# Entry of a SwiGLU FFN: the norm ahead of most weight splits, and the first half's products for two pairs of blocks at the beginning

## The chip, the cores and the metric

One NeuronCore of one Trainium2 chip. The metric is the device time of one execution of the program, in microseconds (us). Three runs of the kernel before took 769.72, 771.16 and 771.29 us; their median is 771.16 us.

## The reference

A decoder layer on 512 tokens of 1024 features, all float32: a norm, a combined projection, two groups of heads (RWKV-7 time mixing and sparse attention), an output projection with a residual, and then a dense SwiGLU FFN of 2816 hidden features with a second residual and a last norm. What the change touches is the seam between the output projection and the FFN:

```python
h = h + jnp.concatenate([y_r, y_n], axis=-1) @ w_out[l]
h = h + swiglu(rms_norm(h, norm_ffn[l]), w_gate[l], w_up[l], w_down[l])
return rms_norm(h, norm_final)

def swiglu(x, w_gate, w_up, w_down):
    return (jax.nn.silu(x @ w_gate) * (x @ w_up)) @ w_down
```

## The kernel before

*Products in three matmuls.* Every float32 product runs as three matmuls on a rounded high part ("hi") and a remainder ("lo") of each operand (`mm3`, L163 to L165). `split` (L144, L146) makes the two parts: hi is a copy by ScalarE (ACT), lo a subtraction by VectorE (DVE).

*Output projection (`accumulate` with `w_out`, L1157).* All eight banks of PSUM hold one output: four tiles of 128 tokens, two banks each, tile 0 in the banks "s", tile 1 in "pj", tile 2 in "ra", tile 3 in "o" and "rb". The last two slices of `w_out` run tile by tile, so that tile 0 is finished first; behind each tile come the residual adds into `x2` (L1159) and one step of the FFN's norm.

*The norm (`ffn_norm`).* For each tile: a sum of squares and a root on ScalarE, a reciprocal and the scaled product on VectorE (L1072), eight transposes on TensorE into two banks of "s" (L1082), and a copy by ScalarE into `raw` (L1084). The tokens are taken in two halves, tiles 0 and 1 against tiles 2 and 3, and the features in two halves too. For tiles 0 and 1 the copied values are split into A11 and A12. For tiles 2 and 3, four sums and differences with the tile of the first half (L1095 to L1097, L1100) and five splits give S1, S2, S3, S4 and A22.

*The weights (`weight_side`).* The 22 blocks of 128 hidden features are done in 11 pairs q. For each pair the 256 columns of `w_gate` and `w_up` are loaded in halves of 512 rows, 512 KB each: b11, b21 (both `w_gate`) and b22 into buffers of the tag "wraw" by SyncE's (SP) queue; t1 and t3 first by SP and then with an accumulating transfer that GpSimd (POOL) issues (L1137, L1138), which adds the other matrix. For odd q, t1 to t3 lie in a buffer of the tag "L", for even q in three of "t4". VectorE adds t2 = t1 + b22 (L1141) and later t2 + b21 (L1146). Seven operands are split for each pair: B11, B21, T2, T1, T3, B22, T4. Their parts go to buffers of the tags "whi" and "wlo" in turn, two of each; those of pair 0 that are made first (two of them) go to "b8".

*The pairs (`prod`, loop over q).* Seven products make the two halves of gate and up for both halves of the tokens: B11 with A11, B21 with A12, T2 with S2, T1 with S1, T3 with S3, B22 with S4, T4 with A22; 24 matmuls of 256 columns each, into banks of "pj", "ra" and "s" in turn. The first two products need only tiles 0 and 1; the other five need all four. VectorE adds up the products (L1187 to L1205), ScalarE takes the Silu.

*Order.* The kernel is written in a layer that decides the order of instructions of each engine itself when the program is built: a planner goes through the instructions in time by its own estimate of their durations, and where several are ready on an engine, program order decides, except that what is traced under `tc.high_priority()` goes ahead. It also gives out the buffers of a tag; an instruction that needs a buffer waits until the last reader of the tile in it is done. On the chip each engine then takes its instructions strictly in the planned order. Before the change the weights' sums, accumulating transfers and splits are under `high_priority`, the norm is not. `ahead()` traces pair 0's weights before the last tiles of the output projection:

```python
def ahead():
    first.append(weight_side(0, 2))

norm = ffn_norm(lambda t: x2[:, t])
for t, banks in accumulate(*jit(...), w_out, 8, ahead):
    for f in range(2):
        sl = slice(f * 512, f * 512 + 512)
        DVE.tensor_add(x2[:, t, sl], banks[f], x2[:, t, sl])
    next(norm)
```

*Buffers.* "L" has four, "b8" six, "t4" four, "t2" three (its tiles: the junk of the sum of squares, the norm's s3, the products' u, g0 and v, and smaller tiles in all stages before), "wraw" three. `raw` and the A operands lie in "L" too.

## Time and profile before

| | us |
|---|---|
| median of three runs | 771.16 |
| the profiled execution | 770.73 |
| its span | 769.0 |
| TensorE busy in the span | 738.6 (96%) |
| VectorE busy | 543.3 (71%) |
| ScalarE busy | 381.5 (50%) |
| POOL busy | 160.0 (21%) |

The profile is of one execution; its times run from the start of the span, and what lies outside of the span is 1.7 us. PE is TensorE's matmuls, PEld its weight loads, DVE VectorE, ACT ScalarE. Matmuls are pipelined, so a row of a single one (0.28 us) is longer than the distance to the next (0.12 us). The output projection runs until about 404 us, the 11 pairs until about 641, `w_down` and the last norm fill the rest. A line such as L146 is that of a helper and stands for many tiles, so rows are told apart by the tile's tag: "L<-L" a split of the norm, "whi<-t", "wlo<-wraw" splits of weights; "t<-L" is s3.

### The profile page before, as it was taken

To read this page: it belongs to the slowest core of one execution; us is meant where nothing else is said; L and a number is where in the kernel's file an instruction comes from. 1 tells how busy PE (TensorE), PEld (TensorE's weight loads), DVE (VectorE), ACT (ScalarE), POOL (GpSimd) and SP (SyncE) were. 2 spreads that over 40 slices of the span, in tenths; PEclk is the share of its full clock that TensorE was granted. 3 is DMA by queue.
4 is the path that set the end of the run, shared out by engine and by line. 5 is a ranking of instruction groups with operands and counts; after the bars stand their busy time and mean duration, and the time that the engine had idled before them with its cause. 6 is when DMAs were issued, how large, how long until landed. Compare 5 with 4: busy or idle time off the path is not lost.

```text
span 769.0 us, 14989 instructions
## 1 busy us (share of the span) xinstructions
PE 738.6 (96%) x6093; PEld 648.1 (84%) x6093; DVE 543.3 (71%) x1052; ACT 381.5 (50%) x652; POOL 160.0 (21%) x258
## 2 busy tenths in 40 slices
PE   8999999998889999999996899999999999999996
PEld 7867888898877878867786899999999998888885
DVE  5488689789768987875659497888695994333235
ACT  7398643224277776676447344444443552233224
POOL 3210054058345542442001102020202000000000
PEclk9999999999989999999998999999999999999998
DMA  7722543100051000321218569696768444322102
GB/s 247 223 82 84 164 110 110 55 2 2 3 219 30 3 1 3 85 83 56 83 55 192 110 176 203 161 223 151 161 159 221 112 153 147 110 68 97 55 1 110
DMA packets 69243, 82.83 MB, mean 108 GB/s; under 512 B 4868, under 2 KB 62806, under 8 KB 69174
## 3 DMA queue, kind: packets, MB, share of 16 engines
q1 hardware_dynamic: 57558, 70.34, 28.5%
q0 software_dynamic: 11616, 11.54, 9.9%
q8 instruction: 48, 0.79, 0.4%
q14 instruction: 21, 0.17, 0.1%
HBM read 79.77 MB, written 2.10 MB: 106 GB/s over the span
## 4 chain that ended last, share of the span: by engine, by line
PE 74%; DVE 15%; DMA 6%; issue 2%; ACT 1%; POOL 0%; SPq 0%; DVEq 0%; POOLq 0%; ACTq 0%
PE ps_ra L165 7%; PE ps_ra L164 7%; PE ps_ra L163 6%; PE ps_pj L165 6%; PE ps_pj L163 6%; PE ps_pj L164 6%; PE ps_s L165 4%; PE ps_s L163 4%; PE ps_s L164 4%; PE ps_o L1001 3%; DVE wlo L146 3%; PE ps_pj L993 2%; DMA L<-in_w_up_dram 2%; DMA wraw<-in_w_up_dram 2%; DMA L<-in_w_gate_dram 2%
## 5 line engine op out<-in xcount | busy, mean ns | idle before, releaser
L144 ACT ACTIVATE whi<-wraw 128x1024 fp32r<-128x1024 f32 (+1 forms) x79 | 78.5, 1033 | 33.2 <-PE ps_s L165 8.2
L146 DVE TENSOR_TENSOR wlo<-wraw,whi 128x1024 fp32r<-128x1024 f32 (+1 forms) x62 | 77.7, 1284 | 14.9 <-ACT whi L144 11.3
L146 DVE TENSOR_TENSOR L<-b,L 128x512 fp32r<-128x512 f32 x24 | 16.2, 691 | 57.1 <-PE ps_rb L164 55.1
L990 POOL TENSOR_SCALAR whi<-whi,m,gates 128x128 f32<-128x128 f32 (+3 forms) x64 | 42.5, 679 | 36.9 <-DVE m L988 28.7
L144 ACT ACTIVATE L<-b 128x512 fp32r<-128x512 f32 x24 | 14.9, 632 | 70.0 <-PE ps_rb L164 65.1
L164 PE MATMUL ps_ra<-wlo,L 128*128 128x256 f32 (+1 forms) x140 | 47.6, 340 | 0.2 <-DVE wlo L146 0.2
L163 PE MATMUL ps_ra<-whi,L 128*128 128x256 f32 (+1 forms) x140 | 47.4, 340 | 0.2 <-ACT L L144 0.2
L165 PE MATMUL ps_ra<-whi,L 128*128 128x256 f32 (+1 forms) x140 | 47.0, 337 | 0.0
L165 PE MATMUL ps_pj<-whi,L 128*128 128x256 f32 (+1 forms) x140 | 46.3, 332 | 0.0
L164 PE MATMUL ps_pj<-wlo,L 128*128 128x256 f32 (+1 forms) x140 | 46.3, 331 | 0.0
L163 PE MATMUL ps_pj<-whi,L 128*128 128x256 f32 (+1 forms) x140 | 45.9, 332 | 0.0
L164 PE MATMUL ps_ra<-L,whi 128*128 128x256 f32 (+2 forms) x128 | 44.3, 346 | 1.0 <-DVE L L146 1.0
L163 PE MATMUL ps_ra<-L,whi 128*128 128x256 f32 (+2 forms) x128 | 44.1, 345 | 0.9 <-ACT L L144 0.9
L165 PE MATMUL ps_ra<-L,wlo 128*128 128x512 f32 (+2 forms) x120 | 41.2, 343 | 0.0
L987 ACT ACTIVATE whi<-whi,m 128x128 f32<-128x128 f32 (+3 forms) x64 | 35.4, 554 | 9.3 <-DVE m L986 8.1
L165 PE MATMUL ps_pj<-L,wlo 128*128 128x512 f32 (+1 forms) x112 | 38.8, 346 | 0.1
L163 PE MATMUL ps_pj<-L,whi 128*128 128x512 f32 (+1 forms) x104 | 36.3, 349 | 0.2 <-ACT whi L144 0.2
L164 PE MATMUL ps_pj<-L,whi 128*128 128x512 f32 (+1 forms) x104 | 35.9, 346 | 0.0
L986 DVE CUSTOM_DVE_ANT_0 whi<-ps_s,negb 128x128 f32<-128x128 f32 (+3 forms) x64 | 29.3, 484 | 5.9 <-PE ps_pj L993 2.5
L1137 POOL DMA_DIRECT2D t<-in_w_up_dram x6 | 7.9, 1322 | 115.1 <-DVE whi L146 50.4
L163 PEld LDWEIGHTS ps_ra<-whi,L 128*128 128x128 f32 x140 | 27.6, 197 | 3.1 <-ACT L L144 0.6
L164 PEld LDWEIGHTS ps_ra<-wlo,L 128*128 128x128 f32 x140 | 27.5, 196 | 3.0 <-DVE wlo L146 0.5
(627 smaller groups left out, 2462.4 us busy)
## 6 DMA issues: line engine op xcount, KB each, us to landing
wraw<-in_w_gate_dram SPq DMA_DIRECT2D x22, 512.0 KB
wraw<-in_w_down_dram SPq DMA_DIRECT2D x11, 1024.0 KB
wraw<-in_w_in_dram SPq DMA_DIRECT2D x9, 1024.0 KB
t<-in_w_up_dram POOLq DMA_DIRECT2D x12, 512.0 KB, 7.4
wraw<-in_w_up_dram SPq DMA_DIRECT2D x11, 512.0 KB
L<-in_w_up_dram POOLq DMA_DIRECT2D x10, 512.0 KB, 8.9
wraw<-in_w_out_dram SPq DMA_DIRECT2D x4, 1024.0 KB
wraw<-in_w_in_dram SPq DMA_DIRECT2D x6, 512.0 KB
```

The lines of the kernel that those rows point to most:

```text
L144: ACT.activation(hi, src, AF.Copy)
L146: (POOL if pool else DVE).tensor_sub(lo, src, hi.bitcast(F32))
L163: PE.matmul(o, lh, rh, start=start, stop=False)
L164: PE.matmul(o, lh, rl, start=False, stop=False)
L165: PE.matmul(o, ll, rh, start=False, stop=stop)
L986: DVE.tensor_tensor_reduce(pr[:, i], pS[:, i], negb[:, S - n:S], scale=-1.0, scalar=3e38, op0=OP.add, op1=OP.min, accum_out=m[:, i, 0:1])
L987: ACT.activation(pr[:, i], pr[:, i], AF.Exp, scale=-1.0, bias=m[:, i, 0:1], accum_out=m[:, i, 1:2])
L990: POOL.tensor_scalar(pr[:, i], pr[:, i], m[:, i, 2:3], gv[:, 1 + b0 + i, h:h + 1], op0=OP.mult, op1=OP.mult)
L993: PE.transpose(pT[:, j], prr[:, x, j * 128:j * 128 + 128], ident)
L1001: PE.matmul(po[q, 2 * g:2 * g + 2], vtok[:, j % (t + 1), b0 + j // (t + 1), g], pTs[:, par, j], start=False, stop=g == 1 and bs[-1] == 1 a ...
L1137: POOL.dma_start(t1, quarter(w_up, 0), accum_op=OP.add)
```

## The change

- The norm's steps and the residual adds in front of them run under `high_priority`. Before the output projection's last tiles only B11 and B21 of pair 0 are prepared; pair 1's B11 and B21 and the rest of pair 0 (T2, T1, T3, B22, T4) are traced behind the norm.
- At the beginning the products of the first half of the tokens (B11, B21) run for pair 0 and pair 1, then the five other products of pair 0, then those of pair 1. From pair 2 on the order is as before.
- A11 and A12 are split straight from PSUM; the copy into `raw` comes behind.
- s3 = a11 - a21 is subtracted by POOL instead of VectorE.
- "t2" has four buffers instead of three; two small tiles of pair 1 change places with it. The scratch for POOL's transfers is halved.

```diff
-    SB_BUFS = {"L": 4, "b8": 6, "t4": 4, "t2": 3, "wraw": 3, "whi": 2, "wlo": 2}
+    SB_BUFS = {"L": 4, "b8": 6, "t4": 4, "t2": 4, "wraw": 3, "whi": 2, "wlo": 2}
...
-                rv = raw[:, kh * HK:kh * HK + HK, tl]
-                ACT.activation(rv, p.rearrange("p (k n) -> p k n", n=128), AF.Copy)
+                rv, pv = raw[:, kh * HK:kh * HK + HK, tl], p.rearrange("p (k n) -> p k n", n=128)
                 if t < 2:
-                    put(("A11", "A12")[kh], rv)
+                    put(("A11", "A12")[kh], pv)
+                ACT.activation(rv, pv, AF.Copy)
...
-                DVE.tensor_sub(s3, a11, a21)
+                POOL.tensor_sub(s3, a11, a21)
...
+    class Weights:
+        def __init__(self, q):
...
+            nc.sync.dma_start(self.b11, quarter(w_gate, 0))
+            nc.sync.dma_start(self.b21, quarter(w_gate, 1))
...
+        def begin(self, tag=None):
+            with tc.high_priority():
+                self.put("B11", self.b11, tag)
+                self.put("B21", self.b21, tag)
+
+        def rest(self):
+            b22 = st([128, 2048], "wraw")[:, 0:1024].rearrange("p (k n) -> p k n", n=256)
...
+            nc.sync.dma_start(t1, self.quarter(w_gate, 0))
+            nc.sync.dma_start(b22, self.quarter(w_up, 1))
+            nc.sync.dma_start(t3, self.quarter(w_up, 0))
+            with tc.high_priority():
+                POOL.dma_start(t1, self.quarter(w_up, 0), accum_op=OP.add)
+                POOL.dma_start(t3, self.quarter(w_up, 1), accum_op=OP.add)
+                DVE.tensor_add(t2, t1, b22)
+                self.put("T2", t2)
+                self.put("T1", t1)
+                self.put("T3", t3)
+                self.put("B22", b22)
+                DVE.tensor_add(t2, t2, self.b21)
+                self.put("T4", t2)
...
     def ahead():
-        first.append(weight_side(0, 2))
+        ws[0] = Weights(0)
+        ws[0].begin("b8")
...
-        for f in range(2):
-            sl = slice(f * 512, f * 512 + 512)
-            DVE.tensor_add(x2[:, t, sl], banks[f], x2[:, t, sl])
-        next(norm)
+        with tc.high_priority():
+            for f in range(2):
+                sl = slice(f * 512, f * 512 + 512)
+                DVE.tensor_add(x2[:, t, sl], banks[f], x2[:, t, sl])
+            next(norm)
...
+    ws[1] = Weights(1)
+    ws[1].begin()
+    ws[0].rest()
+    first_products(0)
+    first_products(1)
+    last_products(0)
+    ws[1].rest()
+    last_products(1)
+    for q in range(2, NF // 2):
+        ws[q] = Weights(q)
+        ws[q].begin()
+        ws[q].rest()
+        first_products(q)
+        last_products(q)
...
-    nc = _bacc.Bacc("TRN2", target_bir_lowering=False, num_devices=1, dynamic_dma_scratch_size=4096)
+    nc = _bacc.Bacc("TRN2", target_bir_lowering=False, num_devices=1, dynamic_dma_scratch_size=2048)
```

`first_products(q)` holds the first two products of the old loop's body with their evictions, `last_products(q)` the other five.

## Rows read from the trace of the kernel before

**Rows 1.** Page, part 2: busy tenths of TensorE in 40 equal slices of the span.

```profile
PE   8999999998889999999996899999999999999996
```

**Rows 2.** Windows: each engine's busy us (instructions), granted clock, DMA share, GB/s.

```profile
400.00:420.00 20.00, 15.81 (x91) 14.15 (x89) 18.52 (x26) 15.17 (x26) 2.62 (x2) 0.83 0.70 171
420.00:440.00 20.00, 15.59 (x111) 14.98 (x112) 9.72 (x14) 8.41 (x11) 2.59 (x2) 0.91 0.61 119
440.00:460.00 20.00, 20.00 (x170) 20.00 (x169) 19.34 (x24) 8.95 (x10) 1.27 (x1) 1.00 0.57 146
...
412.00:414.00 2.00, 2.00 (x11) 2.00 (x11) 2.00 (x5) 0.90 (x2) 0.00 (x0) 0.50 1.01 236
```

**Rows 3.** Chain of waits, 380 to 450 us: start us, us on the chain, what.

```profile
408.66 1.14 DVE t L1146
409.80 0.61 DVE L L146
...
425.23 4.02 DMA L<-in_w_gate_dram
...
429.87 6.13 DMA L<-in_w_up_dram
...
437.22 1.23 DVE whi L146
```

**Rows 4.** Timeline of TensorE: start us, us, instruction, idle time before it, releaser.

```profile
403.65 1.03 PE L1082 MATMUL ps_s<-ident,b 128*128 128x128 f32 x8
...
410.45 0.58 PE L164 MATMUL ps_pj<-L,b 128*128 128x256 f32 x1 [1.85 <-DVE L L146]
...
411.04 0.41 PE L163 MATMUL ps_pj<-L,b 128*128 128x256 f32 x1
411.26 0.41 PE L164 MATMUL ps_pj<-L,b 128*128 128x256 f32 x1
...
438.49 0.39 PE L165 MATMUL ps_pj<-L,whi 128*128 128x256 f32 x1 [2.52 <-DVE whi L146]
...
461.12 0.28 PE L163 MATMUL ps_s<-L,whi 128*128 128x256 f32 x1
```

**Rows 5.** Timeline of VectorE, 400 to 471 us, same columns.

```profile
400.44 1.28 DVE L1072 SCALAR_TENSOR_TENSOR b<-L,ss,t 128x1024 f32<-128x1024 f32 x1 [0.42 <-PE ps_s L1082]
...
403.44 1.22 DVE L146 TENSOR_TENSOR wlo<-t,wlo 128x1024 fp32r<-128x1024 f32 x1
...
406.31 1.22 DVE L146 TENSOR_TENSOR wlo<-wraw,wlo 128x1024 fp32r<-128x1024 f32 x1
407.44 1.22 DVE L146 TENSOR_TENSOR whi<-t,whi 128x1024 fp32r<-128x1024 f32 x1
...
409.71 1.29 DVE L146 TENSOR_TENSOR L<-L 128x512 fp32r<-128x512 f32 x2
...
424.51 0.69 DVE L146 TENSOR_TENSOR b<-L,b 128x512 fp32r<-128x512 f32 x1
...
436.08 1.23 DVE L1141 TENSOR_TENSOR L<-L,wraw 128x1024 f32<-128x1024 f32 x1 [5.09 <-DMA L<-in_w_up_dram]
...
470.83 1.22 DVE L1141 TENSOR_TENSOR L<-L,wraw 128x1024 f32<-128x1024 f32 x1 [3.83 <-DMA L<-in_w_up_dram]
```

**Rows 6.** Timeline of ScalarE, same columns.

```profile
400.00 1.09 ACT L1084 ACTIVATE L<-ps_s 128x512 f32<-128x512 f32 x2 [0.18 <-PE ps_s L1082]
...
437.40 1.06 ACT L144 ACTIVATE wlo<-L 128x1024 fp32r<-128x1024 f32 x1 [3.10 <-DVE L L1141]
```

**Rows 7.** Timeline of POOL, 300 to 480 us, same columns.

```profile
305.68 1.04 POOL L884 TENSOR_TENSOR L<-L,cs 128x512 f32<-128x512 f32 x1 [2.87 <-DVE m L988]
...
462.71 1.29 POOL L1137 DMA_DIRECT2D L<-in_w_up_dram  x1 [7.74 <-DVE t L1205]
```

**Rows 8.** Timeline of SyncE's queue, same columns.

```profile
384.97 0.37 SPq L1121 DMA_DIRECT2D wraw<-in_w_gate_dram  x1
...
454.78 0.37 SPq L1123 DMA_DIRECT2D L<-in_w_gate_dram  x1
```

More of the change, by code (lines that the diff above doesn't have):

```diff
@@ L1172, in prod, with first_products @@
         return o
-    hid = []
-    for q in range(NF // 2):
+    hid, part = [], {}
+    def first_products(q):
         if q % 2 == 0:
-            h4 = st([128, 4, S], "b8") if q < NF // 2 - 1 else st([128, 2, S], "t4")
-        hq = h4[:, q % 2 * 2:q % 2 * 2 + 2]
-        hid += [hq[:, j] for j in range(2)]
-        w = weight_side(q) if q else first[0]
-        u, g0, v, u1 = (st([128, 2, 256], tag) for tag in ("t2", "t2", "t2", ("lora", "smask")[q % 2]))
-        p = prod(w["B11"], A["A11"])
+            part["h"] = st([128, 4, S], "b8") if q < NF // 2 - 1 else st([128, 2, S], "t4")
+        hq = part["h"][:, q % 2 * 2:q % 2 * 2 + 2]
+        hid.extend(hq[:, j] for j in range(2))
+        w = ws[q]
+        u, g0 = st([128, 2, 256], "t2"), st([128, 2, 256], "smask" if q == 1 else "t2")
+        p = prod(w.B11, A["A11"])
         with tc.high_priority():
             ACT.activation(u, p, AF.Copy)
-        p = prod(w["B21"], A["A12"])
+        p = prod(w.B21, A["A12"])
         with tc.high_priority():
@@ L1198, in hybrid_layer @@
             DVE.tensor_add(u1, p, v)
-        p = prod(w["B22"], A["S4"])
+        p = prod(w.B22, A["S4"])
         with tc.high_priority():
@@ L1202, in hybrid_layer @@
         DVE.scalar_tensor_tensor(hq[:, :, 0:256], v, -1.0, g0, op0=OP.mult, op1=OP.mult)
-        p = prod(w["T4"], A["A22"])
+        p = prod(w.T4, A["A22"])
         with tc.high_priority():
```

65 lines of the change are left out of this document (25 added, 40 removed).

## Prediction

> **What bounds the kernel now.** I read the views from coarse to fine. The page's second part comes first: TensorE is at nine tenths nearly everywhere, and around 400 to 440 us its row falls to 6 and 8 (slices 22 and 23 of 40) [rows 1]. The 20 us windows say what that hole is: 15.81 and 15.59 us of busy TensorE in 400 to 440, at granted clocks of 0.83 and 0.91, and 20.00 at 1.00 right behind it; in the hole VectorE is full first (18.52 of 20) and then half idle (9.72) [rows 2]. So the FFN is bound by TensorE once it runs, and its entry is bound by something else.
>
> What that is, the chain of waits tells [rows 3]. Up to the first product's second matmul it runs over VectorE, from one split of weights to the next and the sum for T4 (L1146, 408.66) to a split of the norm (409.80). The end of the hole hangs on a load at 425.23 (4.02 us), an accumulating transfer at 429.87 (6.13 us) and a split at 437.22.
>
> TensorE's timeline shows the holes themselves [rows 4]: the last matmuls of the stage before and tile 1's transposes end some 0.9 us after 403.65, the first product gets going at 410.45 after a last wait of 1.85 us for VectorE, and at 438.49 another wait of 2.52 us ends. Warm matmuls take 0.12 us each (170 in 20 us [rows 2]), those behind the first hole 0.21 (411.04, 411.26): the lower of the two levels of the clock, 0.50 granted in 412 to 414 [rows 2]. The first product of pair 2 starts at 461.12 [rows 4], so that is where pairs 0 and 1 have ended. From there on TensorE is dense, and I count a microsecond won at that point as one won at the end.
>
> What could be had at most: two pairs are 14 products of 24 matmuls, 336 x 0.12 = 40.3 us, and 16 transposes of the tiles 2 and 3 in two groups of some 0.9 us. From the end of tile 1's transposes (403.65 + 0.9 = 404.5) that would end at 446.6, 14.5 us ahead of 461.1.
>
> **The change, part by part.** *Opening.* Today tile 1's A11/A12 come last on VectorE: 409.71, behind T1 at 403.44, T2, B22 (406.31), T3 (407.44) and the sum for T4 [rows 3, 5]. Splits of 128x1024 are 1.13 us apart (406.31, 407.44); two operations of 128x512 take 1.29 us where one takes 0.69, so 0.60 each [rows 5]. Ahead of the norm these are 5 x 1.13 = 5.7 us that now come behind it. The split out of PSUM also takes one ScalarE copy out of the chain (two take 1.09 us, so 0.5 each) [rows 6]. Against that, the bank of "s" is held until the copy, the hi and the lo have all read it, some 0.6 us more; I let these cancel. Tile 1's transposes end at 404.5, a hi (0.5) and a lo (0.6) follow: the first product starts at 405.5 instead of 410.45 (bounds 404.5, where the planner puts those transposes into the stage before, and 407, if one more split of 1.13 us gets in between).
>
> *Four products instead of two.* B11 and B21 of pairs 0 and 1 need tokens of tiles 0 and 1 alone. 4 x 24 x 0.12 = 11.5 us and 1.8 us of transposes, all warm if nothing breaks it: 405.5 + 13.3 = 418.8. What lies beside it on VectorE, from the end of tile 2's norm at 400.44 + 1.2 = 401.6: four lo's of tiles 0 and 1 (2.4), two residual adds of tile 3 (1.2), eight operations of tile 2 (4.8), the norm and eight operations of tile 3 (1.3 + 4.8), B11 and B21 of pair 1 (2.3), T2 (1.1), one eviction (0.6): 18.5 us, to 420.1. So VectorE is as full as TensorE; the norm, which goes first, ends at about 420 instead of 425.1 (bounds 418 and 422). T2 x S2 needs the S2 of tile 3, three operations into its eight, and I take a wait of 1.0 us (0 to 3): pair 0's five other products run from 419.8 to 434.2 (5 x 24 x 0.12 = 14.4). Behind the norm VectorE owes T1, T3, B22, the sum for T4 and T4 (5.7) and nine evictions and products of halves (5.4): 11.1 us in 14.4, so no wait more, but no room either.
>
> *POOL instead of VectorE for s3.* Two subtractions of 128x512. POOL's nearest row is another two-input operation of that size: 1.04 us [rows 7], against 0.60. VectorE gets 1.2 us back, and the overwriting of a21 waits 0.4 us longer per tile, which other splits fill: nothing either way (bounds: 1.2 gained, 1 lost). The Trainium skill speaks against this move: "GPSIMD Engine Reference", section 8, has VectorE about twice as fast at elementwise work and the two sharing SBUF interfaces when VectorE reads two SBUF inputs, as nearly all of its operations here do. By that page an estimate would be 1.4 us for each and some waiting on top, at most 1 us later in all. What weighs more is the queue: POOL also issues the accumulating transfers, and s3 stands behind any of them that waits.
>
> *Weights of pair 0.* Its t1 and t3 come long ahead. Pair 1's b11/b21 take the slot of wraw before pair 0's b22, which moves to about 385, where today pair 1's go [rows 8]; landed by 393 even at the slow load below, it is wanted behind the norm, at about 415: nothing.
>
> *Pair 1's sums.* Its t1, t2, t3 live in a buffer of "L" that raw gives back only when the norm has ended: issue at 425.23 today, as the norm's last split (424.51, 0.69 us) has ended [rows 3, 5]. After: about 420. From there 4.0 us of load and 0.6 us to the accumulating issue [rows 3], or 7.9 us as for pair 3, which loads among other transfers (454.78 to 462.71) [rows 7, 8]; then 6.2 us (429.87 to the sum at 436.08) or 8.1 (462.71 to 470.83) [rows 3, 5, 7]; then the sum, a hi and a lo (1.2 + 1.0 + 1.2) [rows 5, 6]. T2 of pair 1 is there between 420 + 4.6 + 6.2 + 3.4 = 434.2 and 420 + 7.9 + 8.1 + 3.4 = 439.4. Until now nobody waited for this end of the chain but one split behind it in VectorE's order; with pair 1's first products spent early, TensorE has nothing else. Pair 2's loads come into the same microseconds, as buffers of pair 0 fall free, so I take 437, past the middle: a wait of 2.8 us (0 to 5). The Trainium skill points the same way and sharpens it: "DMA: Bandwidth & Descriptors", section "Issuing engines are not separate DMA queues", says that transfers issued by any engine run on the same 16 DMA engines and interleave. The trace agrees as far as 7.9 us beside 4.0 go; by that rule the slow end, 439.4, would hold, pair 2 would start 2.4 us later, and the time would be 764.3.
>
> *Sum.* Pair 1's last five products start at 437.0 and end at 451.4. One hole of such a length costs clock: 17 matmuls at 0.21 instead of 0.12 are 1.5 us; the hole of 2.5 us before 438.49 cost none (1.00 granted behind it), the longer one at the opening did [rows 2, 4]; I take 0.9. Pair 2 then starts at 452.3 instead of 461.1: 8.8 us. The profiled execution took 770.73 us, 0.4 under the median of 771.16: 770.7 - 8.8 = 761.9, 762.4 from the median; I say 762.
>
> *Small things.* One more buffer of "t2" serves the two u and g0 that now live at once; it is also used far ahead of the FFN, and the planner may place work there otherwise: 0, bounds 2 us either way, as TensorE's row has few gaps there to fill or to widen [rows 1]. POOL's scratch is halved: the pairs of accumulating issues in flight are two, no row shows a want of room; 0, or one more accumulating transfer of 6.2 to 8.1 us in series for t3 of an odd pair, which only pair 1 could feel.
>
> **The rivals.**
> *All of it is covered* (757): loads as quick as today's and the planner finds work for the hole. No wait for S2 or T2: 405.5 + 13.3 + 28.8 = 447.6, 13.5 us won. For it speaks that TensorE mixes products today; against it that VectorE's sum is already as long as TensorE's.
> *VectorE in its order* (767): today VectorE stood 5.1 us before the sum at 436.08, with T4's split of pair 0 behind it [rows 5]. The same order with a sum that is there at 436 instead of 434, the slow end: T4's lo 1.2 + 1.2 us later at 438.4, T4 and the five products 17.2 us to 455.6, clock 1.5: 457.1, 4 us won.
> *Slower* (773): on POOL, pair 2's second accumulating issue stands ahead of pair 1's first, and its load waits for a buffer of t4 that pair 0's T4 split gives back, at about 428.5 (420.1, the 5.7 us of splits, 2.7 of evictions). Then 428.5 + 7.9 = 436.4 to issue, 8.1 to land, 3.4 to T2, 14.4 and 1.5: 463.8, 2.7 us lost. It decides once pair 1's accumulating issue comes later than 461.1 - 1.5 - 14.4 - 3.4 - 8.1 = 433.7. For it: POOL waits for whole loads and for buffers now (t1 of pair 3, loading since 454.78, was taken up at 462.71) [rows 7, 8]. Against it: the time between 420 and 433.7 is long.
> *It doesn't do what it says* (771): program order and priority only break ties; if each engine's order comes out as now, with the split of T2 and T1 ahead of tile 1's, only POOL and the extra buffer remain.
>
> **How the numbers follow.** Forecast 0.53, all covered 0.14, VectorE's order 0.20, slower 0.07, no effect 0.06. The range takes in the covered case and the opening's early bound (14.5 us, 756) and, above, VectorE's order with the 2 us of earlier work: 756 to 769. The three runs lie 0.2% apart, so 1.5 us is what can be told from no change. Faster: the first three, 0.87, less a little for the third's tail: 0.86; within 0.2%: 0.06; slower: 0.08.
>
> **What would show it.** Right: the first product's matmuls run from about 405 and the clock stays up to 418; the norm's last split at about 420 with SP's load for L right behind it; one hole of TensorE ahead of pair 1's T2, ended by VectorE or that transfer; pair 2 starting at about 452. Wrong: a start of products after 408, a norm that ends after 423, a POOL queue in which s3 waits for a transfer, or a shift of more than 2 us before 390 us.

## The result, and the profile after

The changed kernel takes 779.09 us (median of four runs, 777.67 to 779.93), the kernel before 771.02 us beside it (four runs, 769.72 to 771.29). The ratio is 1.0106, with a 95% interval from 1.0087 to 1.0125: slower by 8 us, where 9 us less were forecast. The profiled execution after took 779.93 us, its span 778.2; before they were 770.73 and 769.0. In the experiments below single executions of e8, e10 and e12 took far longer (898, 1429 and 3975 us); the ratios leave these out.

To see where 9.2 us went I cut the profiled executions at three points of TensorE's timeline: the last matmul of w_out starts, the first matmul of w_down starts, the last one starts. What lies between the first two is called the FFN stage below. A fourth mark lies inside of it: pairs 0 and 1 are 336 matmuls, and the 337th matmul of the pairs starts 57.7 us after w_out's end before (461.12) and 60.9 after (467.61). The stretch up to it is called the entry.

| profiled execution | w_out ends at | FFN stage | of it the entry | w_down |
|---|---|---|---|---|
| before | 403.4 | 238.9 | 57.7 | 119.5 |
| after | 406.7 | 241.3 | 60.9 | 123.0 |
| difference | +3.3 | +2.4 | +3.2 | +3.5 |

So only 2.4 of the 9.2 us lie where the change was meant to win 8.8, and 6.8 lie in stages whose computation the change leaves as it was. The page's second part of after, TensorE's row in 40 slices, shows the entry in slices 22 to 24, now 8, 8 and 8 where they were 6, 8 and 9 [rows 1]: less deep, and longer.

```profile
PE   6999899998989999999998889999999999999996
```

The windows of after (busy us of PE, PEld, DVE, ACT, POOL; granted clock; DMA share; GB/s) answer [rows 2]. TensorE has more in 400 to 420 than before (17.18 against 15.81) and as much in 420 to 440, but stands 3.4 us in 440 to 460, where it was full. VectorE, full at first before, is at 12.07:

```profile
400.00:420.00 20.00, 17.18 (x90) 14.61 (x89) 12.07 (x15) 11.54 (x19) 2.60 (x2) 0.83 0.31 70
420.00:440.00 20.00, 15.47 (x126) 14.66 (x125) 14.72 (x22) 12.26 (x22) 2.74 (x3) 1.00 0.62 156
440.00:460.00 20.00, 16.56 (x120) 15.73 (x120) 14.51 (x17) 6.84 (x8) 2.58 (x2) 0.91 0.51 95
460.00:480.00 20.00, 20.00 (x171) 20.00 (x171) 14.62 (x17) 9.54 (x11) 2.58 (x2) 1.00 0.99 256
```

TensorE's timeline of after answers [rows 4] (start us, us, instruction, idle time before it and what ended it):

```profile
406.73 0.39 PE L165 MATMUL ps_rb<-whi,L 128*128 128x512 f32 x1
408.08 0.65 PE L1082 MATMUL ps_s<-ident,b 128*128 128x128 f32 x4 [0.96 <-ACT L L1086]
409.51 0.66 PE L1082 MATMUL ps_s<-ident,b 128*128 128x128 f32 x4 [0.78 <-ACT L L1086]
410.94 0.58 PE L163 MATMUL ps_pj<-L,b 128*128 128x256 f32 x1 [0.78 <-ACT L L144]
...
412.53 0.58 PE L164 MATMUL ps_pj<-L,b 128*128 128x256 f32 x1 [0.31 <-DVE L L146]
412.91 0.41 PE L165 MATMUL ps_pj<-L,b 128*128 128x256 f32 x1
...
425.88 1.06 PE L1082 MATMUL ps_s<-ident,b 128*128 128x128 f32 x8 [1.73 <-DVE b L1072]
...
454.14 0.39 PE L163 MATMUL ps_s<-L,wlo 128*128 128x256 f32 x1 [2.18 <-ACT wlo L144]
```

The transposes of tile 1 (408.08, 409.51) wait twice for ScalarE's copy out of the bank of "s" that they are to fill. The first product begins at 410.94, cold (0.41 for a matmul that takes 0.28 warm), and tile 2's transposes stand behind 22 of its matmuls, at 417.18. In the kernel before they stand ahead of it:

```profile
406.70 1.14 PE L1082 MATMUL ps_s<-ident,b 128*128 128x128 f32 x8 [2.01 <-ACT L L1084]
```

ScalarE's timeline of after has the copies that free the banks, the first of tile 0 and the two of tile 1:

```profile
407.44 0.58 ACT L1086 ACTIVATE L<-ps_s 128x512 f32<-128x512 f32 x1
...
412.51 1.20 ACT L1086 ACTIVATE L<-ps_s 128x512 f32<-128x512 f32 x2 [1.13 <-DVE L L146]
```

The first stands behind two splits of pair 1's weights (from 405.53), the other two behind VectorE's lo of tile 1.

VectorE's timeline of after answers [rows 5]:

```profile
408.39 1.22 DVE L146 TENSOR_TENSOR whi<-wraw,whi 128x1024 fp32r<-128x1024 f32 x1
409.52 1.22 DVE L146 TENSOR_TENSOR wlo<-t,wlo 128x1024 fp32r<-128x1024 f32 x1
410.66 1.22 DVE L146 TENSOR_TENSOR whi<-t,whi 128x1024 fp32r<-128x1024 f32 x1
411.79 1.28 DVE L146 TENSOR_TENSOR L<-ps_s,L 128x512 fp32r<-128x512 f32 x2
...
420.05 0.69 DVE L1096 TENSOR_TENSOR L<-L 128x512 f32<-128x512 f32 x1 [5.84 <-POOL t L1095]
...
435.33 0.69 DVE L146 TENSOR_TENSOR b<-L,b 128x512 fp32r<-128x512 f32 x1
```

Splits of weights still stand in front of tile 1's part of A11 and A12 (411.79); VectorE then waits 5.84 us for the s3 that POOL now makes, of which s3 itself is 1.29 us and the rest the late transposes and copies of tile 2 in front of it:

```profile
418.73 1.29 POOL L1095 TENSOR_TENSOR t<-L 128x512 f32<-128x512 f32 x1 [2.22 <-ACT L L1086]
```

And the norm's last split is done at 436.0, not at 420, and not at 425.2 as before [rows 5]. What hangs on that end is in the chain of waits of after (start us, us on the chain, what), which answers [rows 3]:

```profile
436.05 3.85 DMA L<-in_w_gate_dram
...
440.55 1.29 POOL L L1145
441.83 4.96 issue
446.79 6.16 DMA L<-in_w_up_dram
...
453.99 1.05 ACT whi L144
455.09 0.53 PE ps_pj L163
```

raw gives its place in L back at 436.05, pair 1's t1 and t3 are loaded into it, POOL issues the first accumulating transfer at 440.55 and the second 6.24 us later, and TensorE, which has run out of products, starts T3 (454.14) and B22 (455.09) behind it.

### The profile page after: what moved, and what is told of

The parts are those of the page before. It is cut to its first block, busy times and chain, and to the rows that moved or that the text cites. A ratio compares the mean times of both kernels' runs of the same rounds, so it can differ in the third digit from the quotient of the medians.

```text
span 778.2 us, 14976 instructions
## 1 busy us (share of the span) xinstructions
PE 742.6 (95%) x6093; PEld 645.5 (83%) x6093; DVE 539.7 (69%) x1050; ACT 382.8 (49%) x653; POOL 161.3 (21%) x260
## 4 chain that ended last, share of the span: by engine, by line
PE 75%; DVE 12%; DMA 7%; issue 3%; ACT 2%; POOL 1%; SPq 0%; POOLq 0%; ACTq 0%; DVEq 0%
PE ps_pj L165 7%; PE ps_pj L163 7%; PE ps_ra L165 7%; PE ps_ra L164 7%; PE ps_pj L164 7%; PE ps_ra L163 6%; PE ps_s L165 4%; PE ps_s L163 4%; PE ps_s L164 4%; DMA L<-in_w_up_dram 3%; PE ps_o L1001 3%; PE ps_pj L993 2%; DMA L<-in_w_gate_dram 2%; DVE wlo L146 1%; PE ps_s L980 1%
## 5 line engine op out<-in xcount | busy, mean ns | idle before, releaser
L146 DVE TENSOR_TENSOR L<-b,L 128x512 fp32r<-128x512 f32 x24 | 16.3, 692 | 62.6 <-PE ps_rb L164 60.4
L990 POOL TENSOR_SCALAR whi<-whi,m,gates 128x128 f32<-128x128 f32 (+3 forms) x64 | 42.7, 684 | 36.8 <-DVE m L988 28.6
L165 PE MATMUL ps_pj<-whi,L 128*128 128x256 f32 (+1 forms) x140 | 47.2, 338 | 0.0
L163 PE MATMUL ps_pj<-whi,L 128*128 128x256 f32 (+1 forms) x140 | 46.7, 337 | 0.0
L164 PE MATMUL ps_ra<-L,whi 128*128 128x512 f32 (+2 forms) x120 | 41.3, 344 | 0.0
L163 PE MATMUL ps_ra<-L,whi 128*128 128x512 f32 (+2 forms) x120 | 41.1, 342 | 0.0
L165 PE MATMUL ps_pj<-L,wlo 128*128 128x256 f32 (+1 forms) x120 | 40.4, 337 | 0.0
L165 PE MATMUL ps_ra<-L,wlo 128*128 128x512 f32 (+2 forms) x112 | 39.1, 349 | 0.0
L163 PEld LDWEIGHTS ps_pj<-whi,L 128*128 128x128 f32 x140 | 27.0, 193 | 3.7 <-issue 0.8
```

The source lines that it names most:

```text
L146: (POOL if pool else DVE).tensor_sub(lo, src, hi.bitcast(F32))
L163: PE.matmul(o, lh, rh, start=start, stop=False)
L164: PE.matmul(o, lh, rl, start=False, stop=False)
L165: PE.matmul(o, ll, rh, start=False, stop=stop)
L990: POOL.tensor_scalar(pr[:, i], pr[:, i], m[:, i, 2:3], gv[:, 1 + b0 + i, h:h + 1], op0=OP.mult, op1=OP.mult)
```

## The experiments

All with the kernel before on the same chip beside them. First all of them with their three stages, worked out as above from each one's profiled execution, and the column of the shift: by how many bytes, whole multiples of 2048 left out, the tiles behind t2 in SBUF (gin, b8, whi, wlo, kB) start later than in the kernel before.

| kernel | shift | w_out ends | FFN stage | of it the entry | w_down | median us | ratio to before, interval |
|---|---|---|---|---|---|---|---|
| before | 0 | 403.4 | 238.9 | 57.7 | 119.5 | 771.0 | |
| after | 32 | 406.7 | 241.3 | 60.9 | 123.0 | 779.1 | 1.0106 [1.0087, 1.0125] |
| e1 before, t2 of four, scratch halved | 32 | 406.6 | 236.1 | 54.6 | 123.0 | 775.2 | 1.0072 [1.0050, 1.0095] |
| e2 after, A11/A12 split from raw | 32 | 408.3 | 238.6 | 59.4 | 123.0 | 778.6 | 1.0112 [1.0094, 1.0130] |
| e3 after, s3 on VectorE | 32 | 406.6 | 239.3 | 59.5 | 123.0 | 777.6 | 1.0088 [1.0064, 1.0112] |
| e4 after, two banks at first | 32 | 408.7 | 239.0 | 60.1 | 123.0 | 779.6 | 1.0123 [1.0107, 1.0139] |
| e5 before, shifted | 32 | 408.9 | 235.9 | 56.8 | 123.0 | 776.1 | 1.0064 [1.0041, 1.0087] |
| e6 before, scratch halved | 0 | 402.0 | 238.3 | 58.2 | 119.5 | 770.0 | 0.9994 [0.9980, 1.0009] |
| e7 after, shifted | 64 | 407.1 | 239.0 | 60.4 | 120.6 | 776.2 | 1.0081 [1.0054, 1.0108] |
| e8 e7 with e2 to e4 at once | 64 | 407.2 | 234.4 | 56.7 | 120.6 | 771.8 | 1.0024 [1.0003, 1.0044] |
| e9 before, shifted | 64 | 405.2 | 233.8 | 56.8 | 120.6 | 768.1 | 0.9971 [0.9957, 0.9985] |
| e10 e7, pair after pair | 64 | 408.0 | 244.7 | 67.3 | 120.6 | 784.0 | 1.0173 [1.0153, 1.0193] |
| e11 e8, t1 of pair 1 in t4 | 64 | 408.0 | 231.8 | 52.9 | 120.6 | 767.0 | 0.9962 [0.9945, 0.9979] |
| e12 e11, s3 on POOL | 64 | 410.2 | 230.6 | 54.7 | 120.6 | 767.2 | 0.9968 [0.9951, 0.9985] |
| e13 e11, A11/A12 split from PSUM | 64 | 408.3 | 234.4 | 56.3 | 120.6 | 772.3 | 1.0021 [1.0007, 1.0035] |
| e14 e11, three banks at first | 64 | 406.3 | 233.6 | 56.1 | 123.0 | 771.8 | 1.0009 [0.9992, 1.0026] |
| e15 e7, t1 of pair 1 in t4 | 64 | 408.5 | 233.5 | 56.9 | 120.6 | 771.5 | 1.0012 [0.9998, 1.0027] |
| e16 before, shifted | 128 | 404.8 | 237.1 | 57.0 | 122.5 | 773.6 | 1.0049 [1.0030, 1.0067] |
| e17 before, shifted | 96 | 406.5 | 235.5 | 56.8 | 123.0 | 773.9 | 1.0053 [1.0033, 1.0074] |
| e18 e14 once more | 64 | 406.6 | 232.4 | 56.5 | 120.6 | 768.9 | 0.9988 [0.9970, 1.0006] |

Each stage is read from one execution. How far that carries, e14 and e18 show, which are the same kernel: they differ by 1.2 us in the FFN stage and by 2.4 in w_down, but by 0.4 in the entry. Behind the entry TensorE stands up to three times for 0.1 to 1.3 us before a split on VectorE, with the same instructions once in one kernel and not at all in another (e9 0.83 us, e5 none). So the entry says more of the change than the whole FFN stage does, and a difference below 1 us says little.

### The layout alone (e1)

```diff
-"t2": 3, ... dynamic_dma_scratch_size=4096
+"t2": 4, ... dynamic_dma_scratch_size=2048
```

> The kernel before with the fourth buffer of t2 and the halved scratch of POOL, and nothing else of the change. Theory A: the changed kernel loses its time outside of the FFN's entry too, by where its buffers lie or how the planner orders the stages before, namely 2.1 us at the start (the norm's gain lands later) and a slower pace of the 512-column matmuls (0.233 instead of 0.227 us each): then this kernel is 3 to 5 us slower than the one before, about 775, with 87 to 88 matmuls in 20 us of the w_down stage. Rival: these belong to the one profiled execution or chip, and the loss is all of the entry: then 771, with 90 matmuls in 20 us.

775.21 us, 5 us slower than before, with nothing of the change but these two numbers. w_out ends 3.2 us later, w_down takes 3.5 us more, and the FFN stage 2.8 us less. So what I had put down as "0, bounds 2 us either way" holds most of the loss against the kernel before. Which of three things it is, the tiles' places, the halved scratch or another order of instructions (the fourth buffer changes it), this run doesn't tell.

### Three parts of the entry, one at a time (e2, e3, e4)

```diff
 e2: -put(("A11", "A12")[kh], pv)        # ahead of the copy to raw
     +put(("A11", "A12")[kh], rv)        # behind it
 e3: -POOL.tensor_sub(s3, a11, a21)
     +DVE.tensor_sub(s3, a11, a21)
 e4: -ps(("pj", "ra", "s")[turn3[0] % 3], ...)
     +ps(("pj", "ra")[turn3[0] % 2] if turn3[0] < 6 else (as before), ...)
```

> The changed kernel with A11 and A12 split from the copy in raw again instead of from PSUM. Theory B: the split out of PSUM keeps a bank of s through hi, lo and copy one after the other, so tile 1's transposes end at 410.2 instead of 404.5 and tile 2's stand behind the first product: undone, the first product starts about 4 us earlier, tile 2's transposes stand ahead of it as before, the norm ends 5 to 8 us earlier, and the time is 771 to 774. Rival: the opening is bound by the splits of weights that still stand ahead of tile 1's on VectorE (B21, B11, T1, T2): then no more than 1 us, 778.

> The changed kernel with s3 subtracted by VectorE again. Theory B: VectorE stands 5.8 us before its first operation behind s3 because tile 2's transposes are late, and POOL's 1.3 us itself adds 0.8 us for each of two tiles: 777 to 778. Rival: POOL and the pair of engines waiting for each other are the loss: 3 us or more, 776 or less.

> The changed kernel with the first six products in the banks pj and ra alone, so that none of them waits for a bank of s that the norm's transposes hold. Theory C: B11 of pair 1 is the third product, its bank of s is not free before tile 3's copies at 427, and so TensorE stands from 424.0 to 427.2 with work at hand: undone, 2.5 to 3.5 us less, 776. Rival (theory B): tile 3's norm ends as late as before, TensorE only stands later instead, before T1 or T2 of pair 0: within 1 us, 778 to 779.

Each shortens the FFN stage of after by 2.0 to 2.8 us, and the entry by 1.5, 1.4 and 0.8 us. In the whole time only e3 shows something (777.6, 1.5 us less, an interval that overlaps that of after), as its theory B said; e2 and e4 come out where their rivals put them. In e2 and e4 w_out ended 1.5 and 1.9 us later than in after, with the same instructions in the same order up to there: TensorE's granted clock was low for longer in other places (0.50 in 202 to 206 in e2, where after has 0.93; 0.57 in 88 to 92 and in 136 to 140 in e4, where after has 1.00). In e2 tile 2's transposes stand ahead of the first product again, at 411.51, as theory B wanted; the product itself comes no earlier, and the norm ends 1.9 us earlier, both counted from w_out's end. None of the three is the cause by itself.

### Places, scratch, order (e5, e6, e9, e16, e17)

```diff
 e5:  -posci = st([64, 1], "posci", dtype=I32)
      +posci = st([64, 9], "posci", dtype=I32)[:, 0:1]     # e9: 17, e17: 25, e16: 33
 e6:  -dynamic_dma_scratch_size=4096
      +dynamic_dma_scratch_size=2048
```

In all five the instructions and their order on every engine are those of the kernel before; only addresses differ.

> The kernel before with one small tile (posci) made 32 bytes longer, so that every SBUF tile allocated behind it (gin, b8, whi, wlo, kB among them) starts 32 bytes later; L, t4, wraw and t2 stay; the instructions and their order on all five engines are the same. Theory P (the placement of the tiles costs, as the layout alone had cost 5 us): the 128x512 matmuls of w_down slow from 0.2267 to 0.233 us, that stage grows from 119.5 to 123.0 us, w_out by 1.3, the pairs' matmuls get faster by 2 to 3 us in all: about 772 to 775 us. Theory S (the halved scratch of POOL's transfers) and theory O (the other order of instructions that the fourth buffer brings): no change, 770 to 771 us, w_down at 119.5.

> The kernel before with POOL's transfer scratch at 2048 instead of 4096 bytes: all tiles start 2048 bytes earlier, same instructions, same order. Theory P: 2048 is a multiple of any small grain, so no change, 770 to 771 us, w_down at 119.5. Theory S: the late start (gain row landing 2 us later) and part of the 5 us are here: 772 to 775 us. Theory O: no change.

> The kernel before with posci 64 bytes longer: gin, b8, whi, wlo and kB start 64 bytes later, the offset that they have in the shifted changed kernel; same instructions and order as before. Theory P (the placement sets the pace of the matmuls whatever the program): w_down 120.6 us, the pairs' 128x256 matmuls 115 to 118 ns apart instead of 117 to 120, the stage from the end of w_out to w_down 234 to 236 us instead of 238.9; the whole about 767 to 770 us. Rival (the faster pairs come from the other order of instructions): that stage stays at 238 to 239 and the kernel at 771 to 772.

> The kernel before with posci 128 bytes longer; same instructions and order as before. Theory P with a grain of 128 bytes (the offsets that matter repeat after 128): as the kernel before, w_down 119.5 us, the stage from w_out's end to w_down 238 to 239, 769 to 771 us. Theory P with a grain of 64: as the shift by 64, w_down 120.6, the stage 233 to 235, 767 to 769. Rival (the pace is a chance of each build and has nothing to do with offsets): any of the three, and no reason for either.

> The kernel before with posci 96 bytes longer; same instructions and order as before. Theory P with a grain of 64 bytes: as the shift by 32, w_down 123.0 us, the stage from w_out's end to w_down 235 to 237, 774 to 777 us. With a grain of 128: a fourth offset with a pace of its own. Rival (chance of each build): w_down 119.5 or 120.6 as likely as 123.0.

The same program takes 770.4 us unshifted, 776.1 by 32 bytes, 768.1 by 64, 773.9 by 96 and 773.6 by 128; the unshifted kernel beside each of them took 770.0 to 770.4. The two intervals of e5 and e9 don't touch. The halved scratch alone takes 770.0. So theory P holds as far as that the place alone moves the time by 1% with not one instruction changed, and S and O fall as causes of it. A grain of 64 or of 128 bytes falls as well: 128 is neither as 0 (119.5) nor as 64 (120.6). The pace repeats from kernel to kernel: the last 192 matmuls of w_out take 51.0 us in both kernels at shift 0, 52.1 in all six at 32 and 51.3 in all ten at 64. At 32 bytes w_down costs 3.5 us more, w_out 1.1, and each of the pairs 2 to 10, where no stand comes in, takes 19.87 us instead of 20.02: 3.2 us more in all. The rest of e5's 5.7 us isn't located. The whole program starts later in every other profile than in that of before (its first transposes of activations at 7.80 us, in the others at 8.5 to 10.1), so 2.1 of the 3.3 us that w_out ends later in after are no cost of the place.

What e6 does show is in POOL's timeline. With the old scratch the two accumulating transfers of an odd pair go out 1.1 us apart (429.87 on the chain of [rows 3], the next at 430.99). With half of it the second waits until the first is through:

```profile
427.57 1.29 POOL L1137 DMA_DIRECT2D L<-in_w_up_dram  x1 [7.81 <-DVE t L1191]
433.86 1.30 POOL L1138 DMA_DIRECT2D L<-in_w_up_dram  x1 [5.00 <-issue]
```

6.29 us apart. In the kernel before nobody waits for t3 so early; in after it is the 6.24 us between 440.55 and 446.79 on the chain above.

### The change, shifted, and repaired (e7, e8)

```diff
 e7: after, posci as in e5 (net shift 64)
 e8: e7 with the edits of e2, e3 and e4
```

> The changed kernel with posci 32 bytes longer, so that the tiles behind it stand 64 bytes, and not 32, away from their offset in the kernel before (less the 2048 of the scratch); same instructions and order as the changed kernel. Theory P: w_down back from 123.0 to 119.5 us and w_out by 1.3 faster, the pairs 2 to 3 us slower: 775 to 777 us. Theories S and O: 779 us as the changed kernel.

> The changed kernel, shifted as the one before it, with three parts of the entry undone or altered at once: the hi and lo of A11 and A12 read the copy in SBUF again, s3 is back on VectorE, and the first six products use only the banks pj and ra, so that the norm's transposes and the products never want the same bank of s. In the three runs of one part each the stage from the end of w_out to the first w_down product took 238.6, 239.3 and 239.0 us against 241.3 in the changed kernel. If the three gains add (theory: the entry loses at three separate waits), that stage is about 234 to 236 us and the kernel 769 to 772; if they are one and the same wait (theory: one bottleneck, PE's idle time only moves), the stage stays at 238.5 to 240 and the kernel at 773 to 776.

e7: w_down 120.6 us, the whole 3 us less. Against the kernel before at the same shift (e9) its FFN stage is 5.2 us longer (239.0, 233.8), and so it was at the shift of 32 (after 241.3, e1 236.1; e5 235.9). So the FFN stage really lost 5.2 us and not 2.4, which the faster pairs of another place had half hidden. Of these 3.6 lie in the entry (60.4, 56.8), the rest in stands and a changing pace behind it; against e1, which has the fourth buffer too, the entry of after loses 6.3 us.

e8: the three undone at once take 4.6 us off the stage, inside of the range for gains that add, though less than their sum of 7.1; off the entry they take 3.7 us, which is the sum of the three there, as for separate waits. The norm ends 24.3 us after w_out's end instead of 29.1 in e7. TensorE's timeline then has one long stand left:

```profile
446.69 0.58 PE L163 MATMUL ps_ra<-kB,whi 128*128 128x256 f32 x1 [6.36 <-ACT whi L144]
```

It is T1 of pair 1 (with S1, in kB), whose t1 was loaded at 431.94 at the earliest (SP's queue, L1141), when raw had gone. Here the load is slow: pair 2's two loads go out 1.0 and 0.6 us ahead of it, the DMA engines are full from 432 to 438 (shares of 0.92 to 1.09), and POOL issues the accumulating transfer at 439.28, 7.3 us after the load's issue.

### Pair after pair (e10)

```diff
-ws[1] = Weights(1); ws[1].begin(); ws[0].rest()
-first_products(0); first_products(1); last_products(0)
-ws[1].rest(); last_products(1)
+ws[0].rest(); first_products(0); last_products(0)
+ws[1] = Weights(1); ws[1].begin(); ws[1].rest()
+first_products(1); last_products(1)
```

> The shifted changed kernel with the opening in the old order of the text: all seven products of pair 0, then pair 1's first weights, its other weights and its seven products; the split out of PSUM and POOL's s3 stay. Theory G (the loss of the entry is the gate that the norm's end sets on pair 1's sums, whose tiles take raw's place in L: with four products ahead of the norm's second half in PE's queue the norm ends at 436 instead of 425): the norm ends earlier, 426 to 431, pair 2 starts 3 to 6 us earlier, and the stage from w_out's end to w_down falls from 239.0 to 234 to 237 us; the kernel at 772 to 774. Rival (the loss is in the split out of PSUM and in POOL's s3, whatever the order of the products): that stage stays at 238 to 240, the kernel at 775 to 778.

784.0 us, an FFN stage of 244.7 and an entry of 67.3: neither theory. POOL's timeline and VectorE's say why:

```profile
425.23 1.30 POOL L1146 DMA_DIRECT2D t<-in_w_up_dram  x1 [10.19 <-DMA t<-in_w_up_dram]
426.01 1.81 POOL L1095 TENSOR_TENSOR t<-L 128x512 f32<-128x512 f32 x1
```

```profile
427.86 0.69 DVE L1096 TENSOR_TENSOR L<-L 128x512 f32<-128x512 f32 x1 [12.30 <-POOL t L1095]
```

In this order s3 stands in POOL's queue behind an accumulating transfer that waits for its load; VectorE waits 12.30 us for s3, and tile 3's transposes 7.46 us for VectorE. So the run can't judge the order of the products. It shows what the prediction named as the danger of this edit ("s3 stands behind any of them that waits") and priced at nothing.

### The gate on pair 1's t1 (e11, e15)

```diff
-t1, t2, t3 = (tt[:, i] for i in range(3))      # tt in "L"
+t1 = st([128, HK, 256], "t4")                  # for q == 1 alone
+t2, t3 = (tt[:, i] for i in range(2))
```

> The kernel with the three parts undone, and pair 1's t1 in a tile of t4 (which comes free with the norm's gain row, after its last scaling) instead of in raw's place in L. Its load from w_gate can then go out when the last token tile has been scaled, some 6 to 8 us before raw is free. Theory G: PE's stand of 6.36 us before pair 1's T2 goes, or most of it; the stage falls from 234.4 to 228 to 231 us; the kernel at 766 to 769. Rival (the load of t1 is late for another reason, POOL's queue or SP's, or the next wait takes its place): 233 to 235, the kernel at 771 to 773.

> The shifted changed kernel (stage 239.0, 776.1 us) with one edit: pair 1's t1 in a tile of t4 instead of in raw's place in L. Theory G alone (the gate of raw's place in L is what cost the entry): 233 to 235, the kernel at 770 to 772. Rival (the norm's own lateness, from POOL's s3 and the banks, sets the pairs' first sums whichever tile t1 is in): 237 to 239, 774 to 776.

e15 is this one edit in the changed kernel: the FFN stage falls from 239.0 to 233.5, the whole from 776.2 to 771.5, as theory G said. The entry falls from 60.4 to 56.9 us, which is what the kernel before takes at this shift (56.8): what it had lost is gone with one tile in another place, although the norm ends as late as in e7 (29.1 us after w_out's end in both, the last split at 436.90). The other 2.0 us lie behind the entry, where e7 stands three times and e15 once. e11 has it on top of e8: 231.8, 767.0, a little short of what G wanted (228 to 231). SP's queue of e11 shows t1 going out 12 us earlier, and TensorE's timeline what is late next:

```profile
419.87 0.37 SPq L1145 DMA_DIRECT2D t<-in_w_gate_dram  x1
...
432.73 0.47 SPq L1147 DMA_DIRECT2D L<-in_w_up_dram  x1
```

```profile
450.10 0.39 PE L163 MATMUL ps_s<-L,wlo 128*128 128x256 f32 x1 [3.18 <-ACT wlo L144]
```

The stand of 6.36 us before T1 is gone; 3.18 us before T3 are left, whose t3 is loaded into raw's place at 432.73 and accumulated at 442.91, one transfer at a time. e11 is faster than both kernels (3 us under before), but not told apart from e9, the kernel before at the same shift (intervals 0.9945 to 0.9979 and 0.9957 to 0.9985); by the stage it has 2.0 us on it, by the entry 3.9 (52.9 against 56.8; 60.4 in e7). Part of that may be the clock: it was granted 0.97 in 405 to 460 in e11 and 0.91 in e9. The gate and the three parts add up again: 3.5 us (e15) and 3.7 (e8) by themselves, 7.5 together.

### One part put back into the best version (e12, e13, e14, e18)

The edits are those of e2, e3 and e4 the other way, each alone in e11; e18 is e14 unchanged.

> The best version so far (t1 of pair 1 in t4, the three parts undone; stage from w_out's end to w_down 231.8 us, 767.0) with s3 on POOL again, as in the change. Theory Q (POOL's queue: s3 stands in order with the transfers that add one matrix to another, and the next two steps of the norm on VectorE need s3 done): VectorE waits for POOL 1 to 6 us at the line that overwrites a21, the norm ends 2 to 6 us later, and the stage grows to 234 to 237, the kernel to 769 to 772. Rival (a queue with little in it, the prediction's step c): no change, 231 to 233, 766 to 768.

> The best version so far with A11 and A12 split out of PSUM again, as in the change, and the copy to raw behind. Theory R (hi, lo and copy read one bank one after another on two engines, so that the bank comes free later, PE stands longer before tile 1's transposes, and its clock falls): PE transposes tile 1 in two groups of 4, the granted clock is 0.50 from 412 to 418, and the stage grows to 234 to 236, the kernel to 769 to 771. Rival (the split that no longer waits for a copy saves the 0.5 us of the prediction's step a): 231 to 232, 766 to 767.

> The best version so far with the first six products turning over the three banks pj, ra and s again, as in the change. Theory B (the products take a bank of s that the norm's transposes want, in PE's one queue): PE stands 1 to 3 us before tile 3's transposes or before B11 of pair 1, and the stage grows to 233 to 235, the kernel to 768 to 770. Rival (two banks are as tight as three, the products only change who waits): 231 to 232.5, 766 to 768.

> The kernel of e14 once more, unchanged. Its w_down took 122.97 us in the profiled execution, while the seven other kernels with the tiles shifted by 64 bytes took 120.6 each, and its operands in w_down lie at the same addresses as theirs. Theory V (the pace varies from one load of the program to the next): 120.6 us this time. Theory K (the pace belongs to the build: the same kernel has it each time): 123.0 us again, and placement alone does not set it.

e12: no change in the whole time (767.2, stage 230.6): theory Q's price falls. Its waits came: VectorE waits for POOL 1.19 and 2.95 us at L1096, the norm ends 3.1 us later than in e11 (27.4 us after w_out's end against 24.3), and the entry is 1.7 us longer. That the stage is shorter all the same lies behind the entry: e11 stands three times there (0.26, 0.96 and 0.66 us), e12 not once. So the run doesn't show that s3 on POOL costs nothing.

e13: 772.3 us, 5 us slower, the stage 2.6 us and the entry 3.4 us longer: theory R holds, with a whole time somewhat above its range; the profiled executions differ by 3.0 us (772.52, 769.48), and where the other 2 us of the medians are isn't shown. Tile 2's transposes start at 418.40 instead of 411.28, and the norm ends 28.6 us after w_out's end instead of 24.3. The windows of e13 (columns as above), and then those of e11:

```profile
412.00:414.00 2.00, 1.49 (x5) 0.99 (x4) 2.00 (x4) 0.95 (x2) 0.00 (x0) 0.50 0.24 34
414.00:416.00 2.00, 1.86 (x8) 1.86 (x9) 1.81 (x3) 1.19 (x2) 0.00 (x0) 0.50 0.69 228
416.00:418.00 2.00, 2.00 (x11) 2.00 (x11) 0.00 (x0) 0.00 (x0) 1.26 (x1) 0.52 0.36 88
```

```profile
412.00:414.00 2.00, 1.40 (x9) 0.89 (x8) 2.00 (x4) 2.00 (x5) 0.00 (x0) 1.00 0.31 52
414.00:416.00 2.00, 2.00 (x18) 2.00 (x18) 2.00 (x3) 1.99 (x5) 0.00 (x0) 1.00 0.60 210
416.00:418.00 2.00, 2.00 (x20) 2.00 (x18) 2.00 (x6) 0.63 (x1) 1.33 (x1) 1.00 0.21 44
```

With the split out of PSUM TensorE gets through 24 instructions in these 6 us, with the copy first through 47, at the full clock. But the low clock at this place is partly chance, as two executions of one kernel show, which splits from the copy (e14, then e18):

```profile
412.00:414.00 2.00, 1.81 (x8) 1.82 (x9) 2.00 (x4) 2.00 (x6) 0.00 (x0) 0.50 0.71 242
```

```profile
412.00:414.00 2.00, 1.54 (x13) 1.55 (x14) 2.00 (x4) 2.00 (x6) 0.00 (x0) 1.00 0.76 248
```

All seven kernels with the split out of PSUM (after, e3, e4, e7, e10, e13, e15) open at 0.50; of the six with the copy first and products of two pairs, two do (e8, e14). So the late transposes are shown as the price of the split out of PSUM, and how much of e13's loss the clock adds to them is not.

e14: 771.8 us, with a stage only 1.8 us longer and no stand before tile 3's transposes: not theory B as I had put it. Its w_down took 123.0 us, though its operands lie at the same addresses as those of e11, which took 120.6 like the seven other kernels at this shift. e18 is the same kernel again: w_down 120.6, the whole 768.9. So the third bank costs 0.6 to 1.8 us of the stage; of the entry it costs 3.2 and 3.6 us, with a stand of 6.58 us before T3 in both where e11 has 3.18. And the pace of w_down can differ for one kernel from one time to the next: theory V. It can change within an execution too: e14's w_out took 51.3 us as the others' at this shift, and only what came behind was slower. The windows of w_down, one from before, then after, e14 and e18, count the 128x512 matmuls in 20 us (90, 88, 87, 89):

```profile
660.00:680.00 20.00, 20.00 (x90) 16.57 (x89) 7.47 (x8) 6.34 (x8) 0.00 (x0) 1.00 0.23 86
```

```profile
660.00:680.00 20.00, 20.00 (x88) 16.05 (x86) 6.66 (x7) 4.90 (x6) 0.00 (x0) 1.00 0.30 106
```

```profile
660.00:680.00 20.00, 20.00 (x87) 16.22 (x86) 7.49 (x8) 6.34 (x8) 0.00 (x0) 1.00 0.21 68
```

```profile
660.00:680.00 20.00, 20.00 (x89) 16.38 (x89) 7.48 (x8) 6.33 (x8) 0.00 (x0) 1.00 0.31 102
```

## Why the prediction was wrong, step by step

*Where the miss lies.* The sum gave 761.9 us for the profiled execution, and it took 779.9. Of these 18.0 us, 12.0 lie in the entry (60.9 us, where 48.9 had been forecast: 403.4 to 452.3), 3.5 in w_down and 3.3 ahead of w_out's end; the pairs behind the entry gave 0.7 back. So two thirds are *Pair 1's sums*, which were to start at 420 and started at 436.05, when the norm had ended; the steps in front of that are why it ended so late. The other third lies outside: 4.6 us by the term that was put at 0 (w_down 3.5, w_out 1.1 by its pace), and 2.1 by the later start, which no part of the change explains.

*Small things, "0, bounds 2 us either way".* The step that failed outside of the entry. The place of the tiles, moved by 32 bytes through t2's fourth buffer less half of the scratch, costs 5.7 us by itself (e5, 776.1 against 770.4; 3.2 to 6.7 by the interval), and e1, with nothing but the two numbers, 5.1. I had looked for work that the planner might shift, and not at the addresses. The end for the scratch that I named and didn't take ("one more accumulating transfer of 6.2 to 8.1 us in series for t3 of an odd pair, which only pair 1 could feel") is what came: 6.24 us on the chain of after. It was not undone by itself in the entry, so its share there is open; T3's wait of 2.18 us in after and of 3.18 us in e11 stands behind it.

*Opening, 405.5.* Wrong: 410.94, and 412.53 by the mark that the prediction took for before (the second matmul, 410.45). The norm did not get ahead of the splits. Before, five operations stood in front of tile 1's split; after, four (B21 and B11 of pair 1, T1 and T2 of pair 0, the last three at 408.39 to 410.66). On ScalarE two splits of weights stand ahead of tile 0's first copy (407.44) and a third ahead of its second (408.87), and tile 1's transposes wait for both. They are ready, the engine is free, and the planner fills the gap; built without the priority on the norm, the changed kernel has the same order of instructions on every engine, so that line of the change did nothing. That is the rival "it doesn't do what it says", which I gave 0.06, come true for this part. From the end of w_out to the second matmul of the first product TensorE did gain, 5.8 us (406.73 to 412.53) instead of 7.0 (403.42 to 410.45), but the product ran cold in both.

*The split out of PSUM: 0.5 us saved, the bank held 0.6 longer, "I let these cancel".* Wrong by 3.4 us of the entry (e13), and 5 us in the whole time. The copy to raw, and with it the bank, comes behind hi and lo: in after tile 1's copy waits 1.13 us for the lo and starts at 412.51. TensorE gets its transposes in two parts with a wait before each, the clock falls to 0.50 in 412 to 416, and tile 2's transposes come at 417.18, behind most of a cold product; before, and in every run with the copy first, they stand ahead of it.

*Four products warm, the norm done at 420.* Wrong by 16 us (436.0). Tile 2 came late as just said; VectorE stood 5.84 us for an s3 that hung on them; tile 3's scaled product came at 424.46.

*s3 on POOL: nothing either way.* Wrong, somewhat beyond the bound of 1 us: 1.7 us of the entry in e12, where the whole time doesn't show it, 1.4 in after (e3), and 12.30 us of VectorE's time where it is queued behind a waiting transfer (e10). The durations agree with "GPSIMD Engine Reference", section 8, of the Trainium skill (VectorE about twice as fast): 1.29 and 1.41 us on POOL in after, 0.69 on VectorE. The estimate from that page was right there (in e10 and e12 single ones took 1.81 to 3.41), and the queue mattered more, as the sentence behind it said.

*Pair 1's sums.* The chain was the right one, link by link, and its lengths too: load 3.85 us (I had 4.0), accumulation 5.93 and 6.16 (6.2). What it lacked is its last link: in after TensorE waits not for T2 but for T3, behind the second of the two transfers in series. The slow end that the Trainium skill's "DMA: Bandwidth & Descriptors" ("Issuing engines are not separate DMA queues") pointed to was not reached in after; e8, with pair 2's loads beside it, came near it (7.3 us, where 7.9 had been taken). But the chain began at 436.05 instead of 420. My rival "slower" (0.07) had set the point from which it decides, pair 1's accumulating issue later than 433.7; it came at 440.55. I had the mechanism as a rival and let it hang on POOL's order, when the norm's end was enough. e15, which changes nothing but the buffer of that one t1, takes back 3.5 us of the entry and 4.7 of the whole time.

*What would show it wrong.* All four signs came, or nearly: products behind 408, a norm that ends behind 423, 2.2 us of delay at 340 and 2.9 at 390, and (in e10) s3 behind a transfer. The third of them I misread at first: the first transposes of the kernel start 2.1 us later in after because the gain row lands later. They start 1.6 us later in e6 as well, which is as fast as before; so that delay at the start belongs to no part of the change.

*What the idea is worth.* With the gate lifted and the parts repaired, four products at the opening give 2.0 to 3.2 us of the FFN stage against the kernel before at the same shift (e11, e12 against e9), 2.1 to 3.9 of the entry, not 8.8; in the whole time they are not told apart from it. What is left in the way is T3 (3.18 us), the four splits that the planner puts ahead, and 2.0 us before tile 2's transposes, which the kernel before has as well. A version with the whole scratch and one that holds the splits back by a dependency were not tried.

## What to carry to other kernels

A consumer that is moved forward meets the end of the longest chain of its last input: follow that chain back to who frees its buffer, and give that tile another place before moving the products. Priorities break ties and hold nothing back: what is ready goes into every gap. And before the parts of a change are argued over, run the kernel before with the change's buffers alone: a change of layout that costs 1% hides any gain of that size.

## What the runs showed of the hardware that was not expected

- Moving tiles in SBUF by 32, 64, 96 or 128 bytes, with the same instructions in the same order, changed the whole time from 770.4 to 776.1, 768.1, 773.9 and 773.6 us. w_down, all dense 128x512 matmuls at a granted clock of 1.00, took 119.5, 123.0, 120.6, 123.0 and 122.5 us; the pairs' 128x256 matmuls were faster at every shift than unshifted (a pair in 20.02, 19.87, 19.55, 19.84 and 19.90 us). Which tile's offset it is, and how, stays open. The pace is not fixed by the offset alone: one kernel showed 123.0 us once and 120.6 once (e14, e18).
- With 2048 instead of 4096 bytes of scratch POOL issued a 512 KB accumulating transfer only when the one before was through: 6.3 us apart instead of 1.1 (e6 against before).
- The granted clock behind a gap was not the same for like gaps: after a stand of 2.0 us before tile 2's transposes it was 0.50 in 412 to 414 in e8 and 1.00 in e11, and in two executions of one kernel 0.50 (e14) and 1.00 (e18); behind stands of 0.96, 0.78 and 0.78 us (after) and of 0.98, 0.78 and 0.32 us (e13) with transposes between them it was 0.50 for some 6 us.
